# Moving loop, softmax and output operands to other offsets modulo 256 bytes, and one rotation from GpSimd to VectorE, in a hybrid attention block

## The chip, the cores and the metric

The kernel runs on one core of a Trainium2 chip. The metric is the device time of one execution in microseconds. Three timed executions of the kernel before took 802.62, 804.39 and 804.96 us, a median of 804.39 us. One more execution was recorded by the hardware profiler; it took 802.8 us, of which 801.0 us lie between the first and the last instruction (the span).

## The reference, cut to what matters

The block normalises x (512 tokens, 2048 columns), projects it with one matrix `w_in`, runs two groups of attention heads on the result, gates the heads' outputs with a SiLU, multiplies by `w_out`, adds x and normalises once more.

```python
h = _rmsnorm(x, norm_g[l])
proj = h @ w_in[l]
...
qa = _rope(_heads(qa, N_HEADS_A, HEAD_DIM_A))
kc = _compress(_rope(kca), cmp_k_pos, cmp_k_w1, cmp_k_w2)
vc = _compress(vca, cmp_v_pos, cmp_v_w1, cmp_v_w2)
o_a = gates[0] * o_cmp + gates[1] * o_sel + gates[2] * o_win
y_a = o_a * silu(za)
...
o_b = _banded_attention(qb, _rope(kb), vb, WIN_B, sink)
y_b = o_b * silu(zb)
x = x + concatenate([y_a, y_b]) @ w_out
return _rmsnorm(x, final_g)
```

Group A has 8 heads of 128 columns (compressed, selected and window attention), group B 16 heads of 64 columns with a window of 128 tokens and a sink. All products are float32.

## The kernel before

**How a product is made.** A float32 operand is kept as two words, a high one (`h`, rounded) and the remainder (`l`). `mm3` (L118 to L121) makes one product out of three matmuls: high by high, then high by low, then low by high; the scheduler may change their order. A matmul streams its second operand (the moving one, 256 or 512 columns here) past its first operand (the stationary one, 128 columns), which a weight load has put into the array before. A `pe.transpose` is a matmul too: it streams the identity `ident` (128 columns) past the tile that is transposed.

**The stages, in order of time.** Projection of group B and its attention (to 291 us): matmuls of 512 columns that stream `xh`/`xl` past weight words, and between them the scores (L349, L350), transposes (L384) and outputs (L389, L390) of `softmax_b` and `attn_b`. The value loops: for u in 0 to 3, `tok_chunk` (256 columns, weights moving, x stationary) makes the values of `wv1`, and after each chunk come two `compress_unit` calls of 8 matmuls each (L708, L709; weights moving, `F` stationary); then for u in 0 to 7 the same with 280 columns of `wv0` and one `compress_unit`. Then `seven` (L570 on) makes each head's query and gate from seven half-size products of 256 columns (`prod`, L551): the x words `pu`, `qw`, `xh`, `xl` move, the weight words stand still. Eight heads follow each other; `attn_a` of head h (scores L932, transposes L969, L981, L983, outputs L975 to L977, L990, L992) is interleaved by the scheduler with the products of `pair(h + 1)`. Last, from about 620 us, the product with `w_out`: the words of y stand still and the weight words move (L1153 on and `product`, L1254).

**Where the words lie.** `words(place)` gives a pair of weight words out of tiles of 1088 columns; `place` shifts the use inside the tile, so that the 1024 columns used begin at another offset. `MOVING, EVEN, STILL, BELOW = 0, 16, 32, 48` columns are 0, 64, 128 and 192 bytes. Adding up the tiles in the order of their pools gives each operand's address; the table has it modulo 256 bytes.

| operand | before | after |
|---|---|---|
| weight words at MOVING / EVEN / STILL / BELOW | 128 / 192 / 0 / 64 | the same, BELOW no longer used |
| `xh`, `xl`, `pu`, `qw` | 192 | 192 |
| `KH`, `KL` (from their first column) | 192 | 192 |
| `qh`, `ql`, `qs` | 0 | 0 |
| `ident` | 128 | 192 |
| `F`, `ph`, `pl`, `pcr`, `pd` | 128 | 192 |
| `VH`, `VL`, `VC`, `VF`, `VB`, `tt0`, `tt1`, `pc`, `ttb` | 192 | 0 |
| words of y (`yh`, `yl`, and `p`, `q`, `u` of `combos`) | 192 | 0 |

In what follows **the step** from one matmul to the next is the address of the next stationary operand minus the address of the current moving operand, modulo 256 bytes. Inside each loop of the kernel before the step is 64: the value loops have 192 - 128, `compress_unit` 128 - 64, the heads' products 0 - 192, an attention output 192 - 128, the output stage 192 - 128.

**The single steps.** `step` (L125 to L127) issues one matmul of 256 columns at the end of a stage whose result is overwritten; its operands are chosen by address alone. There are three: before the value loops (L828), through `seven` in `keys(0)` (L635) and before the last part of the output stage (L1168).

**Head 0's rotation.** `pair(h)` (L671) takes the query half of `seven`, rotates it in `turn` (L658 to L666: two half products and a product on VectorE, then an addition) and splits it in `q_split` (L257: high word on ScalarE, low word a subtraction). For h below 6 the addition (L664) and the subtraction (L261) run on GpSimd. The query tile `t1` has one buffer, so the next head's first write into it, the ScalarE copy at L608, follows the subtraction.

Of the kernel before, what the change touches and what calls it, by code (L numbers as in the profile page):

```python
# [27 lines left out]
CMP = 32  # L28
MOVING, EVEN, STILL, BELOW = 0, 16, 32, 48
WARM = 40  # L30
# [5 lines left out]
def hybrid_block(ctx, tc, xT, xtm, w0, wv0, wv1, wz, wq, wo0, wos, cw1, cw2, cpos, e2, rope, tabs, sinks, gT, fg, out):  # L36
# [5 lines left out]

    const = ctx.enter_context(sb("const"))
    wp = ctx.enter_context(sb("wp", bufs=3))
    ident = const.tile([P, P], F32, name="ident")
# [4 lines left out]
    bmask = tab[:, 512 + NQ * CMP:768 + NQ * CMP]  # L50
    small = const.tile([P, 8], F32, name="small")
    rstd, eps = small[:, 0:NQ], small[:, NQ:NQ + 1]
    rstdb = const.tile([P, S], F32, name="rstdb")
    gates = const.tile([P, NQ, 24], F32, name="gates")
    gt = const.tile([P, KT + 1], F32, name="gt")
    rowvalid = gt[:, KT:KT + 1]

# [49 lines left out]
    xpool = ctx.enter_context(sb("xpool", side="right"))  # L107
    xh = xpool.tile([P, KT, S], F32R, name="xh")
    xl = xpool.tile([P, KT, S], F32R, name="xl")
    angles = xstack.enter_context(sb("angles", side="right"))  # L110
# [11 lines left out]

    flat = xh.rearrange("p k s -> p (k s)")

# [19 lines left out]
    def load_x(k):  # L144
        xr = tmp("xr")
        if k == 0:
            nc.sync.dma_start(gt, gT)
        nc.sync.dma_start(xr, xT[:, k, :])
        last["xh"] = act.activation(xh[:, k, :], xr, AF.Copy, scale=gt[:, k:k + 1]).ins
        return xr  # L150
# [48 lines left out]
    with tc.issue_after(last["dma"]):  # L199
        nc.sync.dma_start(cosB, rope[:, 2, :])  # L200
        nc.sync.dma_start(sinB, rope[:, 3, :])
        nc.sync.dma_start(tab, tabs)
    dve.tensor_tensor(out=cosB, in0=cosB, in1=rstdb, op=ALU.mult)
    dve.tensor_tensor(out=sinB, in0=sinB, in1=rstdb, op=ALU.mult)
# [86 lines left out]

    vbf = wb.tile([P, NQ, P], F32, name="vbf")
    sk = wb.tile([P, 5, 16], F32, name="sk")
    nc.sync.dma_start(sk[:, 0, :], sinks)
    act.activation(sk[:, 1, :], sk[:, 0, :], AF.Copy, scale=-1.0)
    KBH = wb.tile([P, 2, S], F32R, name="KBH")
    KBL = wb.tile([P, 2, S], F32R, name="KBL")
    VB = wb.tile([P, NQ, 2, P], F32R, name="VB")
# [34 lines left out]
    def softmax_b(i, q2):  # L333
        g = i // 4
        tts = []
        skb = sk[:, 0, 2 * i:2 * i + 2].unsqueeze(1).to_broadcast([P, 2, 2])
        nskb = sk[:, 1, 2 * i:2 * i + 2].unsqueeze(1).to_broadcast([P, 2, 2])
        for part in range(2):
            sums = wk.tile([P, 3, 2, 2], F32, name="sums", tag="sums")
            mn, dn, ex = sums[:, 0], sums[:, 1], sums[:, 2]  # L340
            for e in range(2):
                qt = 2 * part + e
                tt = wb.tile([P, 2, 256], F32, name="ttb", tag="ttb", bufs=6)
                tts.append(tt)
                ko = max(qt - 1, 0) * P
                qs = slice(qt * P, (qt + 1) * P)
                sp = pssb.tile([P, 2, 256], F32, name="spb", tag="spb")
                for v in range(2):
                    pe.matmul(sp[:, v, :], q2[v][:, qs], KBH[:, g, ko:ko + 256], start=v == 0, stop=False)  # L349
                    pe.matmul(sp[:, v, :], q2[v][:, qs], KBL[:, g, ko:ko + 256], start=False, stop=v == 1)  # L350
                n = 256 if qt else 128
                for v in range(2):
                    dve.tensor_tensor_reduce(out=tt[:, v, 0:n], in0=sp[:, v, 0:n], in1=bmask[:, 256 - n:256],
                                             scale=-SCALE_B, scalar=1e38, op0=ALU.add, op1=ALU.min,
                                             accum_out=mn[:, e, v:v + 1])
            dve.tensor_tensor(out=mn, in0=mn, in1=nskb, op=ALU.min)  # L356
            dve.tensor_tensor(out=ex, in0=mn, in1=skb, op=ALU.add)
            act.activation(ex, ex, AF.Exp)
            for e in range(2):
                n = 256 if part or e else 128  # L360
                for v in range(2):
                    tv = tts[2 * part + e][:, v, 0:n]
                    act.activation(tv, tv, AF.Exp, bias=mn[:, e, v:v + 1], scale=-1.0, accum_out=dn[:, e, v:v + 1])  # L363
            dve.tensor_tensor(out=dn, in0=dn, in1=ex, op=ALU.add)
            dve.reciprocal(dn, dn)
            for e in range(2):
                n = 256 if part or e else 128
                for v in range(2):
                    tv = tts[2 * part + e][:, v, 0:n]
                    dve.tensor_scalar(tv, tv, dn[:, e, v:v + 1], None, op0=ALU.mult)  # L370
        return tts
# [124 lines left out]
    VF = kv.tile([P, 2, 2, 256], F32, name="VF")  # L496
    VC = [kv.tile([P, P], F32R, name=f"VC{g}") for g in range(2)]
    ahead = ExitStack()
    quarters = [ahead.enter_context(sb(f"ahead{e}", side="right")).tile([P, 1024], F32, name=f"ahead{e}") for e in range(2)]
# [171 lines left out]
    def pair(h, hooks=None, extra=None):  # L671
        def q_done(qv):
            turn(qv, engine=pool if h < 6 else dve)
            return q_split(qv, pool if h < 6 else dve)

# [142 lines left out]
    early, ready = quarters[:1], quarters[1:]  # L818
    places = [words(MOVING), words(BELOW), words(BELOW)]

# [24 lines left out]
    for u in range(8):  # L845
# [5 lines left out]
        if u == 0:  # L851
# [3 lines left out]
            cacc[1] = bank(4)  # L855
        compress_unit(1, u, cacc[1], words(BELOW))
        if 1 <= u <= 3:
# [28 lines left out]
    kv = kvstack.enter_context(sb("kvK", side="right"))  # L886
    KH, KL = [kv.tile([P, CMP + 1056], F32R, name=f"K{e}")[:, 0:CMP + 1024] for e in "HL"]
    for e, k in enumerate((KH, KL)):
        act.activation(k[:, 0:CMP], k0w[:, e].bitcast(F32), AF.Copy)
# [19 lines left out]
    def attn_a(h, qh, ql, st):  # L909
# [4 lines left out]
        for pair in range(2):  # L914
            tt = wa.tile([P, 1792 if pair else 768], F32, name=f"tt{pair}", tag=f"tt{pair}")
            sums = wk.tile([P, 2, 2, 3], F32, name="sums", tag="sums")
            mn, dn = sums[:, 0], sums[:, 1]
# [82 lines left out]

    yh, yl = [[w[:, (2 * f + 1) % 17, :] for f in range(16)] for w in (xh, xl)]

# [148 lines left out]
    for c, u, ms in ((0, 0, ()), (0, 1, ()), (0, 2, ()), (1, 0, (0, 1, 2)), (1, 1, (3, 4)), (1, 2, (5, 6)), (0, 3, ()),  # L1151
                     (1, 3, (7,))):
        hi, lo = load_unit(wo0[:, c, u], 1024, place=MOVING, loaded=first_units.pop(0) if first_units else None, after=last["qh"],  # L1153
                           after_lo=low_y[11] if (c, u) == (0, 2) else last["turn"])
# [9 lines left out]
        with tc.issue_after(words_of), tc.issue_after(last["gate", 1]):  # L1164
            for m in ms:
                combos(m)
    banks1 = banks(1)
    step(banks1[3], flat[:, 3 * S - 16:3 * S + 112], flat[:, 2 * S + 32:2 * S + 288])  # L1168
    for T in range(2):
# [30 lines left out]
    def halves(raw, to=None):  # L1200
        hi, lo = to or words(MOVING)
        split_to(hi, lo, raw)
# [6 lines left out]
    for n in range(1, 4):  # L1209
# [117 lines left out]
        else:  # L1327
# [8 lines left out]
            def pair():  # L1336
                return words(MOVING)

# [181 lines left out]
```

## Time and profile before

| what | us |
|---|---|
| timed executions, median (lowest to highest) | 804.39 (802.62 to 804.96) |
| the profiled execution / its span | 802.8 / 801.0 |
| TensorE busy in matmuls | 789.6 (99%), 5693 matmuls |
| weight loads | 739.1 (92%) |
| VectorE / ScalarE / GpSimd | 686.3 / 504.7 / 108.3 |
| DMA | 131.05 MB, mean 164 GB/s |

A profile page has one line for each engine's busy time, 40 slices of the span, the chain of work that ended last, and groups of instructions with the mean duration of one. Further views are used below: windows (busy time and number of instructions between two times), timelines (start, duration, engine, line, operation, written tile <- read tiles, shape), and waits. Matmuls are pipelined: one of 256 columns is shown with a duration of about 0.28 us, and the next one starts 0.11 to 0.12 us after it. So a window counts about two matmuls more than start in it, and the distance between starts, not the duration, is what a matmul costs.

### The profile page before, as it was taken

What the parts mean: (1) busy time and instruction counts of PE and PEld (TensorE: products, weight loads), DVE (VectorE), ACT (ScalarE), POOL (GpSimd) and SP (SyncE); (2) the same over time, 40 slices, a digit from 0 to 9 for tenths busy, and PEclk for the clock granted to TensorE, in tenths of its full rate; (3) what the DMA queues carried; (4) which work ended last, traced back from release to release, by engine and by line L of the source; (5) the groups of instructions that cost most, each with busy time, mean ns of one, the idle gap of its engine ahead of it and who ended that gap; (6) DMA issues with size and microseconds to landing.
All of it is one profiled execution on the core that took longest, in us unless ns stands there. A gap on an engine that the chain in (4) does not pass through costs nothing.

```text
span 801.0 us, 15316 instructions
## 1 busy us (share of the span) xinstructions
PE 789.6 (99%) x5693; PEld 739.1 (92%) x5693; DVE 686.3 (86%) x1407; ACT 504.7 (63%) x1103; POOL 108.3 (14%) x111
## 2 busy tenths in 40 slices
PE   9999999999999999999999999999999999999996
PEld 8788888888888899999999999999999999999996
DVE  7668988889989597759999999998999798978895
ACT  6646657655666356664447778777777867553545
POOL 3615002110121000323210110110100000000000
PEclk9999999999999999999999999999999999999998
DMA  7572243564373469887723213225216836797845
GB/s 239 172 242 81 79 144 106 171 171 150 101 210 106 158 200 281 257 269 194 207 82 106 68 53 119 82 92 159 71 50 216 296 120 219 257 266 193 258 86 211
DMA packets 49563, 131.05 MB, mean 164 GB/s; under 512 B 6000, under 2 KB 8848, under 8 KB 49488
## 3 DMA queue, kind: packets, MB, share of 16 engines
q1 hardware_dynamic: 43376, 110.89, 42.3%
q0 software_dynamic: 5824, 18.65, 10.5%
q8 instruction: 45, 0.74, 0.4%
q10 hardware_dynamic: 288, 0.52, 0.2%
q14 instruction: 30, 0.25, 0.1%
HBM read 113.23 MB, written 16.81 MB: 162 GB/s over the span
## 4 chain that ended last, share of the span: by engine, by line
PE 86%; DVE 6%; DMA 3%; ACT 2%; issue 2%; POOL 0%; SPq 0%; DVEq 0%; ACTq 0%
PE pj L119 16%; PE pj L121 15%; PE pj L120 15%; PE oa L120 5%; PE oa L119 5%; PE oa L121 5%; PE sp L932 4%; PE bank L121 2%; PE bank L120 2%; PE bank L119 2%; DMA xr<-xT 2%; DVE wlo L543 2%; PE tp L969 2%; PE tp L384 2%; DMA raw<-wq 1%
## 5 line engine op out<-in xcount | busy, mean ns | idle before, releaser
L119 PE MATMUL pj<-xh,whi 128*128 128x256 f32 (+1 forms) x592 | 196.9, 333 | 0.6 <-ACT t L608 0.5
L121 PE MATMUL pj<-xh,wlo 128*128 128x256 f32 (+1 forms) x592 | 196.2, 331 | 0.0
L120 PE MATMUL pj<-xl,whi 128*128 128x256 f32 (+1 forms) x592 | 196.1, 331 | 0.0
L119 PEld LDWEIGHTS pj<-xh,whi 128*128 128x128 f32 x592 | 111.4, 188 | 11.0 <-ACT t L608 0.9
L121 PEld LDWEIGHTS pj<-xh,wlo 128*128 128x128 f32 x592 | 111.4, 188 | 10.1
L120 PEld LDWEIGHTS pj<-xl,whi 128*128 128x128 f32 x592 | 111.4, 188 | 9.7
L543 DVE TENSOR_TENSOR wlo<-raw,whi 128x1024 fp32r<-128x1024 f32 (+2 forms) x80 | 92.9, 1172 | 7.8 <-ACT whi L542 7.2
L542 ACT ACTIVATE whi<-raw 128x1024 fp32r<-128x1024 f32 (+2 forms) x80 | 77.6, 985 | 30.7 <-DVE raw L581 11.5
L99 DVE TENSOR_TENSOR wlo<-raw,whi 128x1024 fp32r<-128x1024 f32 (+1 forms) x61 | 72.1, 1184 | 22.8 <-ACT whi L97 22.3
L97 ACT ACTIVATE whi<-raw 128x1024 fp32r<-128x1024 f32 (+1 forms) x60 | 56.6, 945 | 28.8 <-PE pj L120 14.8
L120 PE MATMUL oa<-wlo,xh 128*128 128x256 f32 x200 | 55.5, 278 | 0.0
L119 PE MATMUL oa<-whi,xh 128*128 128x256 f32 x200 | 55.4, 278 | 0.0
L121 PE MATMUL oa<-whi,xl 128*128 128x256 f32 x200 | 55.2, 276 | 0.0
L121 PE MATMUL pj<-pu,wlo 128*128 128x256 f32 x160 | 45.0, 281 | 0.5 <-DVE wlo L543 0.5
L119 PE MATMUL pj<-pu,whi 128*128 128x256 f32 x160 | 45.1, 282 | 0.4 <-DVE zr L581 0.4
L120 PE MATMUL pj<-pu,whi 128*128 128x256 f32 x160 | 44.7, 279 | 0.0
L289 DVE TENSOR_TENSOR pl<-tp,ph 128x512 fp32r<-128x512 f32 (+1 forms) x64 | 40.7, 651 | 3.1 <-ACT ph L288 2.9
L288 ACT ACTIVATE ph<-tp 128x512 fp32r<-128x512 f32 (+1 forms) x64 | 34.1, 560 | 9.6 <-PE tp L969 4.4
L363 ACT ACTIVATE ttb<-ttb,sums 128x256 f32<-128x256 f32 (+1 forms) x64 | 30.0, 471 | 14.4 <-DVE sums L356 14.4
L121 PEld LDWEIGHTS oa<-whi,xl 128*128 128x128 f32 x200 | 37.6, 188 | 0.0
L120 PEld LDWEIGHTS oa<-wlo,xh 128*128 128x128 f32 x200 | 37.6, 188 | 0.0
L119 PEld LDWEIGHTS oa<-whi,xh 128*128 128x128 f32 x200 | 37.5, 188 | 0.0
(401 smaller groups left out, 2369.8 us busy)
## 6 DMA issues: line engine op xcount, KB each, us to landing
raw<-wq SPq DMA_DIRECT2D x41, 512.0 KB, 4.4
raw<-wz SPq DMA_DIRECT2D x36, 512.0 KB, 4.0
cw<-cw SPq DMA_DIRECT2D x32, 256.0 KB, 4.0
raw<-wos SPq DMA_DIRECT2D x14, 512.0 KB, 5.9
rw<-wos SPq DMA_DIRECT2D x10, 512.0 KB, 4.8
xr<-xT SPq DMA_DIRECT2D x16, 256.0 KB, 3.4
rows<-xT SPq DMA_DIRECT2D x8, 512.0 KB, 4.7
raw<-wo SPq DMA_DIRECT2D x8, 512.0 KB, 6.0
```

The source lines that it names most:

```text
L97: last["hi"] = act.activation(hi[:, :width], rw[:, :width], AF.Copy).ins
L99: last["lo"] = dve.tensor_tensor(out=lo[:, :width], in0=rw[:, :width], in1=hi[:, :width].bitcast(F32), op=ALU.subtract).ins
L119: pe.matmul(ps, ah, bh, start=first, stop=False, skip_group_check=go_on)
L120: pe.matmul(ps, ah, bl, start=False, stop=False, skip_group_check=go_on)
L121: recent["mm"] = pe.matmul(ps, al, bh, start=False, stop=last, skip_group_check=go_on).ins
L288: act.activation(ph, tp, AF.Copy)
L289: dve.tensor_tensor(out=pl, in0=tp, in1=ph.bitcast(F32), op=ALU.subtract)
L363: act.activation(tv, tv, AF.Exp, bias=mn[:, e, v:v + 1], scale=-1.0, accum_out=dn[:, e, v:v + 1])
L384: pe.transpose(tp[:, o:o + P], tts[kt + s][:, v, c0:c0 + P], ident)
L542: split_hi = act.activation(hi, src, AF.Copy).ins
L543: last["lo"] = dve.tensor_tensor(out=lo, in0=src, in1=hi.bitcast(F32), op=ALU.subtract).ins
L932: pe.matmul(sp[:, a:b], qq[:, qs], kk[:, ko:ko + b - a], start=pi == 0, stop=pi == 2)
```

## The change

It has three parts.

1. Tiles get another size, another order or padding, so that the addresses in the table above go from the left column to the right one. `compress_unit` gets its words at MOVING rather than BELOW, and the output stage at EVEN rather than MOVING. The third `step` gets other operands. `vbf` shares a buffer with `ob`. With that the steps between a loop and the work that interrupts it become 64 as well: products and attention outputs, products and transposes, value chunks and compress units.
2. `rowvalid` moves from the tile `gt` to `small` and gets a DMA of its own (128 rows of 4 bytes on SyncE's queue, after the one of `tabs`).
3. In `pair`, head 0's addition (L664) and subtraction (L261) go from GpSimd to VectorE.

```diff
-MOVING, EVEN, STILL, BELOW = 0, 16, 32, 48
+MOVING, EVEN, STILL = 0, 16, 32
...
+    gt = const.tile([P, KT], F32, name="gt")
...
-    small = const.tile([P, 8], F32, name="small")
+    small = const.tile([P, 16], F32, name="small")
...
-    gt = const.tile([P, KT + 1], F32, name="gt")
-    rowvalid = gt[:, KT:KT + 1]
+    rowvalid = small[:, 8:9]
...
-    xh = xpool.tile([P, KT, S], F32R, name="xh")
-    xl = xpool.tile([P, KT, S], F32R, name="xl")
+    slabs = xpool.tile([P, 2 * KT * S + 64], F32R, name="x")
+    xh, xl = [slabs[:, e * KT * S:(e + 1) * KT * S].rearrange("p (k s) -> p k s", s=S) for e in range(2)]
...
+        nc.sync.dma_start(rowvalid, gT[:, KT:KT + 1])
...
-    vbf = wb.tile([P, NQ, P], F32, name="vbf")
+    vbf = wb.tile([P, NQ, P], F32, name="vbf", tag="ob")
+    KBH = wb.tile([P, 2, S], F32R, name="KBH")
+    KBL = wb.tile([P, 2, S], F32R, name="KBL")
     sk = wb.tile([P, 5, 16], F32, name="sk")
...
-            sums = wk.tile([P, 3, 2, 2], F32, name="sums", tag="sums")
+            sums = wk.tile([P, 6, 2, 2], F32, name="sums", tag="sums")
...
     VC = [kv.tile([P, P], F32R, name=f"VC{g}") for g in range(2)]
+    kv.tile([P, 48], F32, name="space")
...
-            turn(qv, engine=pool if h < 6 else dve)
-            return q_split(qv, pool if h < 6 else dve)
+            turn(qv, engine=pool if 0 < h < 6 else dve)
+            return q_split(qv, pool if 0 < h < 6 else dve)
...
-    places = [words(MOVING), words(BELOW), words(BELOW)]
+    places = [words(MOVING) for n in range(3)]
...
-        compress_unit(1, u, cacc[1], words(BELOW))
+        compress_unit(1, u, cacc[1], words(MOVING))
...
     KH, KL = [kv.tile([P, CMP + 1056], F32R, name=f"K{e}")[:, 0:CMP + 1024] for e in "HL"]
+    kv.tile([P, 16], F32, name="space")
...
-    yh, yl = [[w[:, (2 * f + 1) % 17, :] for f in range(16)] for w in (xh, xl)]
+    yh, yl = [[slabs[:, (e * KT + (2 * f + 1) % 17) * S + 16:][:, 0:S] for f in range(16)] for e in range(2)]
...
-        hi, lo = load_unit(wo0[:, c, u], 1024, place=MOVING, loaded=first_units.pop(0) if first_units else None, after=last["qh"],
+        hi, lo = load_unit(wo0[:, c, u], 1024, place=EVEN, loaded=first_units.pop(0) if first_units else None, after=last["qh"],
...
+    cmb.tile([P, 48], F32, name="space3")
     banks1 = banks(1)
-    step(banks1[3], flat[:, 3 * S - 16:3 * S + 112], flat[:, 2 * S + 32:2 * S + 288])
+    step(banks1[3], flat[:, 2 * S:2 * S + P], flat[:, 3 * S - 16:3 * S + 240])
...
-        hi, lo = to or words(MOVING)
+        hi, lo = to or words(EVEN)
...
             def pair():
-                return words(MOVING)
+                return words(EVEN)
```

More of the change, by code (lines that the diff above doesn't have):

```diff
@@ L121, in mm3 @@
         recent["mm"] = pe.matmul(ps, al, bh, start=False, stop=last, skip_group_check=go_on).ins
-    flat = xh.rearrange("p k s -> p (k s)")
+    flat = slabs[:, 0:KT * S]
     def step(bank, still, moving):
@@ L146, in load_x @@
         if k == 0:
-            nc.sync.dma_start(gt, gT)
+            nc.sync.dma_start(gt, gT[:, 0:KT])
         nc.sync.dma_start(xr, xT[:, k, :])
@@ L295, in hybrid_block @@
     act.activation(sk[:, 1, :], sk[:, 0, :], AF.Copy, scale=-1.0)
-    KBH = wb.tile([P, 2, S], F32R, name="KBH")
-    KBL = wb.tile([P, 2, S], F32R, name="KBL")
     VB = wb.tile([P, NQ, 2, P], F32R, name="VB")
@@ L915, in attn_a @@
             tt = wa.tile([P, 1792 if pair else 768], F32, name=f"tt{pair}", tag=f"tt{pair}")
-            sums = wk.tile([P, 2, 2, 3], F32, name="sums", tag="sums")
+            sums = wk.tile([P, 4, 2, 3], F32, name="sums", tag="sums")
             mn, dn = sums[:, 0], sums[:, 1]
```

## The prediction

> **What bounds the kernel now.** The page first, then the stages as windows.
>
> ```profile
> span 801.0 us, 15316 instructions
> PE 789.6 (99%) x5693; PEld 739.1 (92%) x5693; DVE 686.3 (86%) x1407; ACT 504.7 (63%) x1103; POOL 108.3 (14%) x111
> ...
> 291.10:320.40 29.30, 29.30 (x252) 29.29 (x251) 24.16 (x68) 18.89 (x45) 0.87 (x1) 1.00 0.87 260
> 390.40:429.00 38.60, 38.08 (x329) 37.68 (x328) 38.08 (x58) 19.11 (x31) 4.43 (x4) 1.00 0.39 112
> 429.00:620.00 191.00, 190.79 (x1602) 188.66 (x1601) 180.41 (x389) 148.31 (x371) 16.30 (x10) 1.00 0.32 104
> 620.00:678.70 58.70, 58.70 (x510) 58.43 (x509) 49.52 (x127) 43.78 (x105) 0.00 (x0) 1.00 0.60 215
> ```
>
> The columns of a window are its length, then busy time and instructions of TensorE, its weight loads, VectorE, ScalarE and GpSimd, then granted clock, DMA share and GB/s. TensorE is busy 99% of the span and at clock 1.00 in these stages. So time is won only where matmuls follow each other faster, or where one of its few waits goes (the one that the change touches stands below, under head 0). How fast they follow is not the same everywhere:
>
> ```profile
> 298.30:303.50 5.20, 5.20 (x46) 1.00 0.96 316
> 678.80:786.00 107.20, 107.20 (x948) 1.00 0.74 209
> ```
>
> Both hold matmuls of 256 columns alone, at the same clock. A window counts about two more than start in it. The second gives 107.20 / 946 = 113.3 ns a matmul, the first 5.20 / 44 = 118 ns. I call these the **fast** and the **slow spacing**; they differ by 4.5 ns (4%). Both stretches have steps of 64 throughout, so the step alone does not choose between them. The timeline shows what switches:
>
> ```profile
> 303.48 0.28 PE L121 MATMUL bank<-whi,xl 128*128 128x256 f32 x1
> 303.60 0.29 PE L708 MATMUL pj<-whi,F 128*128 128x256 f32 x1
> ...
> 304.07 0.28 PE L708 MATMUL pj<-whi,F 128*128 128x256 f32 x1
> ...
> 305.32 0.28 PE L709 MATMUL pj<-wlo,F 128*128 128x256 f32 x1
> 305.43 0.28 PE L119 MATMUL bank<-whi,xh 128*128 128x256 f32 x1
> ```
>
> From 304.07 to 305.32 eleven matmuls take 1.25 us: 114 ns, fast. Before 303.48 the value chunk was slow, and after 305.43 the next one is slow again. At 303.48 the step is 0 (from `whi` at 128 to `F` at 128), at 305.32 it is 128 (from BELOW at 64 to `xh` at 192). Reading all such places with settled neighbours from the timeline (the first at 295.88, the last at 572.38): a step other than 64 changes the spacing in 12 cases of 13, while steps of 64 kept a fast stretch fast 1914 times of 1914. So **the spacing is something that steps of 64 keep and other steps flip**, and the three `step` matmuls (own steps 0 and 128, and at 291.11 entered from 512 columns) each set it to fast. Mean durations per group carry the same mark:
>
> ```profile
> L120 PE MATMUL bank<-wlo,xh 128*128 128x256 f32 x62 | 17.4, 281 | 0.0
> L121 PE MATMUL oa<-whi,xl 128*128 128x256 f32 x137 | 37.8, 276 | 0.0
> L121 PE MATMUL pj<-xh,wlo 128*128 128x256 f32 x200 | 56.1, 281 | 0.0
> L975 PE MATMUL op<-ph,VH 128*128 128x256 f32 x50 | 14.1, 282 | 0.0
> ```
>
> 276 ns is the fast spacing (row two, window 678.8 to 786), 281 the slow one: row one is the value chunks (291.1 to 320.4), rows three and four are products and outputs in the heads' stage (429 to 620).
>
> **The change part by part**, against the profiled execution's 802.8 us.
>
> *Value loops (291 to 320).* 250 matmuls start there: at 113.3 ns they would need 28.4 us of the 29.3; 0.8 us is lost to the slow spacing. After the change chunk and `compress_unit` have steps of 64 on both sides, so the fast spacing set at 291.11 should last. One matmul in this stage waited:
>
> ```profile
> 298.12 0.34 PE L120 MATMUL bank<-wlo,xh 128*128 128x256 f32 x1
> 298.30 0.28 PE L121 MATMUL bank<-whi,xl 128*128 128x256 f32 x1
> ```
>
> It takes 180 ns to the next start, 60 too many; if that drops the spacing to slow, the remaining 190 stay slow with nothing to flip them back. Ends: 0.8 gained; 250 x 4.5 = 1.1 spent where 0.8 was, 0.3 lost. I take **-0.5**, nearer to the gain, because the next chunks' spacing decides most.
>
> *The 280-column loop (320 to 353).* A matmul of 280 columns ends 96 bytes further modulo 256, so its spacing drifts by itself. Only the 64 compress matmuls can gain: 0.2 us at most, or lose as much. **-0.1**.
>
> *Heads' stage (429 to 620).* Products are interrupted by outputs (steps 0 in, 128 out), transposes (0 in, 128 out) and scores. 1282 matmuls of 256 columns start there; those that do not follow a wait or a transpose lose 3.2 us to the slow spacing and to settling. The change makes the visits to outputs and transposes 64 both ways. Outputs then no longer flip anything. Transposes are different:
>
> ```profile
> 429.30:434.40 5.10, 5.10 (x47) 1.00 0.60 182
> 487.95:493.10 5.15, 5.15 (x45) 1.00 0.61 206
> ...
> 648.66 0.38 PE L969 MATMUL tp<-ident,tt 128*128 128x128 f32 x2
> 648.80 0.36 PE L120 MATMUL oa<-wlo,xh 128*128 128x256 f32 x1
> 649.00 0.28 PE L121 MATMUL oa<-whi,xl 128*128 128x256 f32 x1
> ```
>
> The first two are long stretches that begin after scores: about 45 and 43 matmuls, at 113 and 119 ns, so one fast and one slow. The matmul behind transposes starts the next one 200 ns later, and the spacing it lands in looks like a coin: of 57 stretches whose entry can be read in this stage (the first at 429.30, the last at 615.25), 25 begin fast, 32 slow. Eight visits in the output stage, between 620.68 and 663.59, already had steps of 64 on both sides of the transposes: 3 landed fast, 4 slow, 1 unreadable. So I keep the coin, let each stretch hold the spacing with which it began, and get 445 slow matmuls x 4.5, 39 in stretches too short to read x 4 and 25 settlings x 8 ns: 2.4 us where 3.05 (scores left out) were. **-0.65**. Ends: all fast, -3.2; all slow, 1200 x 4.5 = 5.4 where 3.2 were, +2.2. Scores into the second column group of `KH` keep their step of 192; that is not changed.
>
> *First output units (620 to 678).* Here the step from scores to products goes from 128 to 192. With 128, five landings of six were fast; with 192, in the heads' stage, 9 of 17. Three stretches of about 45 lose half their chance: **+0.25** (ends -0.45, all of what is lost there now, and +1.5).
>
> *Rest of the output stage.* Fast now; the new third `step` has the same steps around it (0 in, 128 out) and the form of the one at 390.43, which entered from a slow stretch and left fast. **0**; if it failed, 946 x 4.5 = +4.2.
>
> *Group B (74 to 291).* The 182 matmuls of 256 columns lose 0.7 us now. Scores L349 keep their entry step of 64 and are mostly slow with it (118 ns); outputs L389 get the same entry. **0**, ends -0.7 and +0.3.
>
> *`rowvalid`'s DMA, `vbf` in `ob`'s buffer, the padding.* One more issue on SyncE's queue at 50 us, behind which weight loads run a unit ahead; `rowvalid` is read after 350 us, and `ob` is first written a head later than `vbf` is read. **0**; at worst one issue late, under 0.1.
>
> *Head 0 on VectorE.*
>
> ```profile
> 416.61 1.28 POOL L664 TENSOR_TENSOR t<-t,t 128x512 f32<-128x512 f32 x1 [21.54 <-DVE t L662]
> 418.64 1.49 POOL L261 TENSOR_TENSOR ql<-t,qh 128x512 fp32r<-128x512 f32 x1 [0.75 <-ACT qh L260]
> ...
> 414.63 1.23 DVE L543 TENSOR_TENSOR wlo<-raw,whi 128x1024 fp32r<-128x1024 f32 x1
> 415.77 0.69 DVE L662 TENSOR_TENSOR t<-t,cosA 128x512 f32<-128x512 f32 x1
> 416.70 2.27 DVE L543 TENSOR_TENSOR wlo<-raw,whi 128x1024 fp32r<-128x1024 f32 x1
> 418.90 1.78 DVE L677 TENSOR_TENSOR zr<-zr,rstdb 128x512 f32<-128x512 f32 x1
> ...
> 421.25 0.36 ACT L608 ACTIVATE t<-pj 128x256 f32<-128x256 f32 x1
> ...
> 420.85 0.29 PE L932 MATMUL sp<-KH,ql 128*128 128x288 f32 x1
> 421.66 0.39 PE L119 MATMUL pj<-xh,whi 128*128 128x256 f32 x1 [0.52 <-ACT t L608]
> ```
>
> TensorE starts nothing between 420.85 and 421.66: 0.81 instead of 0.13 us, 0.68 lost, until L608 has copied. L608 stands on ScalarE behind the SiLU that waits for L677. While GpSimd works, VectorE's subtraction takes 2.27 instead of 1.23 us and L677 1.78 instead of 0.69: 2.1 us of stretching. The change gives VectorE two instructions of 128x512 at 0.69 us, 1.4 us. The subtraction there waits for ScalarE's high word (0.64 us after the addition); L543 fits between them, and L677 and the sums of the next head stand behind. L677 then ends at about 420.68 - 2.1 + 1.4 = 420.0, L608 at about 420.95, when TensorE is just done. The stall goes: **-0.6**. The other end: the stretching has another cause and stays. Then L677 and all behind it are 1.4 us late in a stage in which VectorE is busy 38.08 of 38.60 us, and the stall grows by as much, +1.4.
>
> Sum: -0.5 - 0.1 - 0.65 + 0.25 - 0.6 = **-1.6 us**. The four executions shown lie at 802.62, 802.8, 804.39 and 804.96; the profiled one is a low one, and the middle of the four is 803.6. I put the new time at 803.6 - 1.6 = **802.0 us**, 0.3% under the median given; the gain itself is 0.2%.
>
> **The rivals.**
> 1. *Transposes keep the spacing too*, once all steps around them are 64. Then the heads' stage stays fast from the `step` at 390.43 except behind scores: -2.6 there, -0.8 and -0.2 in the loops, -0.2 in the first output units, -0.6 for head 0: -4.4, **799.2**. For it: steps of 64 kept the spacing in every settled case. Against it: the eight visits above.
> 2. *Addresses have no effect*, and the two spacings have another cause (what is written, or the queue). Then only head 0 counts: **803.0**. For it: the stretches at 429.30 and 487.95 have the same steps and are fast and slow, so something beside the step takes part. The Trainium skill speaks for this: SBUF — State Buffer, section "A bandwidth-pool intuition that's wrong (but worth ruling out)", gives TensorE a second, independent read port for weight loads, so where the two operands lie should not matter; and TensorE: Matmul & The Clock Gate, section "Back-to-back issue gap", has one isolated spacing for 256 columns, 256 / 2.4 + 2.5 = 109 ns as an estimate. The trace does not agree with one spacing: it has 113.3 and 118 at clock 1.00, and the flips stand where the addresses jump.
> 3. *The last `step` lands slow.* Slower than before: nothing flips the spacing back before 786 us, so +4.2 - 1.6 = +2.6, **806.2**. It decides from the first dozen matmuls after it. For it: these operands have not run in this place. Against it: three of three steps with 128 out led to fast.
>
> **How the numbers follow.** Forecast 0.50, rival 1 0.25, rival 2 0.15, rival 3 0.10. A measurement tells 0.3%, 2.4 us, from no change. The coin of some 57 stretches, each 20 matmuls x 4.5 ns, spreads by 0.7 us, with the long ones and a reordered schedule by about 1.2; so a quarter of the forecast's cases gain over 2.4 us (0.12), with nearly all of rival 1 (0.24): faster 0.36. Slower: most of rival 3 and a little of the rest, 0.09. Same 0.55. The range leaves out rival 3 and the deepest cases of rival 1: **798.8 to 805.0**.
>
> **What would show it.** Windows of the value loops: 250 matmuls in 28.4 us and group means of 276 ns; no flip at the borders of L708. Outputs L975 with the same mean as the products around them. Stretches after transposes still half slow (else rival 1). No wait for L608 at about 421 us, no GpSimd rows there, L543 at 1.2 us. The window after the third `step` at 113.3 ns. The forecast is wrong if the value loops keep 281 ns, or if the heads' stage moves by more than 2 us either way.

## The result and the profile after

The changed kernel took 813.49 us (median of four executions, 812.11 to 817.96), the kernel before 804.38 beside it. The ratio is 1.0127, with a 95% interval of 1.0084 to 1.0169. The prediction said 802.0 us and a range of 798.8 to 805.0: it is wrong by 11.5 us and in sign. Six more executions (run `e11_change_again` below) had a median of 811.75 us, ratio 1.0097 [1.0076, 1.0118].

The profile page of the changed kernel, its first lines and the shares of the chain that ended last:

```profile
span 816.2 us, 15335 instructions
...
PE 799.2 (98%) x5693; PEld 744.1 (91%) x5693; DVE 681.9 (84%) x1409; ACT 504.3 (62%) x1103; POOL 105.0 (13%) x109
...
PE 59%; DVE 22%; DMA 7%; ACT 6%; issue 5%; SPq 0%; POOL 0%; ACTq 0%; POOLq 0%; DVEq 0%
```

The profiled execution is the slowest of the four (817.96). VectorE has less busy time than before (681.9 for 686.3), yet its share of the chain rose from 6% to 22%: TensorE now waits for it. The same line of the kernel before:

```profile
PE 86%; DVE 6%; DMA 3%; ACT 2%; issue 2%; POOL 0%; SPq 0%; DVEq 0%; ACTq 0%
```

The windows say where TensorE waits (columns as in the prediction):

```profile
429.00:620.00 191.00, 187.35 (x1556) 183.22 (x1555) 173.52 (x376) 142.57 (x355) 15.95 (x10) 1.00 0.30 95
620.00:678.70 58.70, 58.46 (x497) 57.87 (x497) 46.54 (x117) 41.70 (x102) 0.00 (x0) 1.00 0.56 196
696.00:786.00 90.00, 90.00 (x766) 90.00 (x765) 75.13 (x89) 44.31 (x61) 8.55 (x10) 1.00 0.75 205
```

Row one, the heads' stage: TensorE stands idle for 3.65 us where it was 0.21, and 46 fewer of its matmuls fit (1556 for 1602). VectorE is busy for 173.52 instead of 180.41 us in the same length, so it stands idle for longer as well (17.5 us for 10.6). Row three is the output stage: 90.00 us for 764 starts are **117.8 ns** a matmul, the slow spacing, where before had the fast one throughout. The waits view of TensorE (waited for, us in total, times, longest) names the rest:

```profile
PE pj L121 <- DVE wlo L545: 2.0, 4, 0.8
PE pj L119 <- ACT whi L544: 1.2, 2, 0.8
...
PE pj L119 <- ACT x L1050: 1.1, 1, 1.1
...
PE oa L120 <- DVE wlo L1055: 0.7, 1, 0.7
```

(L544 and L545 are the weight words' split, L542 and L543 before; L1050 and L1055 make y words, L1047 and L1052 before.)

**How I count.** Two sums are used below, both from the starts of all matmuls in a trace. *Waits*: where the next start comes more than 45 ns later than the length of the matmul asks for (229 ns for 512 columns, 130 for 288, 129 for 280, 115.5 for 256, 109 for 128, and 87 more for the first one behind matmuls of 128 columns), that excess, from 60 us on. *Slow spacing*: what each unbroken stretch of 256-column matmuls takes over 113.3 ns a matmul. For before they are 5.6 and 5.2 us, for the changed kernel 15.5 and 10.3. So 9.9 of the 15.2 us of longer span are waits and 5.1 are slow spacing, 4.3 of these in one stretch. Not all of the waits come with the change. Up to the scores of head 0 (420.2 us in before) TensorE's row is the same in all traces of this document, and the waits there vary from about 3 to 6 us (before 3.7, the change 5.5). From there on before has 1.8 us and the change 9.7.

**Where the waits come from.** The scheduler, which lays out every engine's instructions from its own estimate of their times, gave the changed program another order from head 0 on (424 us). TensorE's row is that of before for the first 2543 matmuls. Of the whole rows, the longest part that stands in the same order in both is 90% on TensorE, 87% on VectorE and 88% on ScalarE. The timeline shows what that means. Head 1's scores before the change:

```profile
445.40 0.38 PE L932 MATMUL sp<-KH,qh 128*128 128x288 f32 x1
445.62 0.29 PE L932 MATMUL sp<-KL,qh 128*128 128x288 f32 x1
445.75 0.28 PE L121 MATMUL pj<-pu,wlo 128*128 128x256 f32 x1
...
446.77 0.28 PE L121 MATMUL pj<-pu,wlo 128*128 128x256 f32 x1
446.89 0.29 PE L932 MATMUL sp<-KH,ql 128*128 128x288 f32 x1
```

and after it, with GpSimd's two rows for the same head:

```profile
443.19 2.13 POOL L666 TENSOR_TENSOR t<-t,t 128x512 f32<-128x512 f32 x1 [45.90 <-DVE t L664]
446.06 2.08 POOL L262 TENSOR_TENSOR ql<-t,qh 128x512 fp32r<-128x512 f32 x1 [0.74 <-ACT qh L261]
...
447.66 0.29 PE L935 MATMUL sp<-KL,qh 128*128 128x288 f32 x1
448.20 0.40 PE L935 MATMUL sp<-KH,ql 128*128 128x288 f32 x1 [0.25 <-POOL ql L262]
448.82 0.39 PE L979 MATMUL op<-pl,VH 128*128 128x256 f32 x1 [0.22 <-DVE pl L290]
```

In the old order ten products stood between the second score and the third, which needs the low word `ql` that GpSimd makes last. In the new one the third score follows at once and waits for `ql`, then the output waits for `pl`, while products that need neither stand behind them. TensorE takes its matmuls in the order given. The Trainium skill states that too (TensorE: Matmul & The Clock Gate, section "The mechanism": matmuls start and end strictly in order), and the rows agree: 0.54 and 0.62 us from start to start instead of 0.13.

The longest wait is at the end of the heads:

```profile
675.85 2.26 ACT L1054 ACTIVATE ph<-yp 128x256 fp32r<-128x256 f32 x7 [2.74 <-PE op L995]
678.01 1.05 ACT L1054 ACTIVATE whi<-raw 128x1024 fp32r<-128x1024 f32 x1
678.96 1.94 ACT L1054 ACTIVATE uh<-yp 128x256 fp32r<-128x256 f32 x6
...
680.12 0.28 PE L121 MATMUL pj<-whi,x 128*128 128x256 f32 x1
...
680.80 0.61 ACT L1050 ACTIVATE x<-yp 128x512 fp32r<-128x512 f32 x1
...
681.47 0.39 PE L119 MATMUL pj<-whi,x 128*128 128x256 f32 x1 [1.06 <-ACT x L1050]
```

Head 7's outputs end at 675.8 us, and ScalarE then has 14 copies ahead of the y word that TensorE wants at 680.2. Before, ScalarE had as many ahead of that word:

```profile
664.23 2.26 ACT L1051 ACTIVATE ph<-yp 128x256 fp32r<-128x256 f32 x7 [1.67 <-PE op L992]
666.40 2.25 ACT L1051 ACTIVATE uh<-yp 128x256 fp32r<-128x256 f32 x7
668.55 0.62 ACT L1047 ACTIVATE xh<-yp 128x512 fp32r<-128x512 f32 x1
```

But 33 matmuls of the output units stood between the last outputs and the product with that word (664.0 to 667.8 us), and TensorE never waited for it. Now there are 3.

**Where the 4.3 us come from:**

```profile
694.49 0.28 PE L121 MATMUL oa<-whi,pl 128*128 128x256 f32 x1
695.46 0.39 PE L120 MATMUL oa<-wlo,x 128*128 128x256 f32 x1 [0.69 <-DVE wlo L1055]
695.68 0.28 PE L121 MATMUL oa<-whi,x 128*128 128x256 f32 x1
```

The third `step`, 49 matmuls earlier, had set the fast spacing (5.59 us for these 49, 114 ns). The stretch behind this wait is slow, and with steps of 64 and no wait behind it all its 957 matmuls stay so: 957 x 4.5 ns = 4.3 us.

### The profile page after: what moved, and what is told of

The parts are those of the page before. It is cut to its first block, busy times and chain, and to the rows that moved or that the text cites. A ratio compares the mean times of both kernels' runs of the same rounds, so it can differ in the third digit from the quotient of the medians.

```text
span 816.2 us, 15335 instructions
## 1 busy us (share of the span) xinstructions
PE 799.2 (98%) x5693; PEld 744.1 (91%) x5693; DVE 681.9 (84%) x1409; ACT 504.3 (62%) x1103; POOL 105.0 (13%) x109
## 3 DMA queue, kind: packets, MB, share of 16 engines
q0 software_dynamic: 5824, 18.65, 10.4%
## 4 chain that ended last, share of the span: by engine, by line
PE 59%; DVE 22%; DMA 7%; ACT 6%; issue 5%; SPq 0%; POOL 0%; ACTq 0%; POOLq 0%; DVEq 0%
PE pj L121 9%; PE pj L119 9%; PE pj L120 9%; PE oa L120 4%; PE oa L121 4%; PE oa L119 4%; DVE wlo L545 3%; PE bank L120 3%; PE bank L121 3%; PE bank L119 2%; PE sp L935 2%; DMA yw<-st 2%; DVE wlo L99 2%; DMA raw<-wq 2%; DVE qs L330 2%
## 5 line engine op out<-in xcount | busy, mean ns | idle before, releaser
L119 PE MATMUL pj<-x,whi 128*128 128x256 f32 (+1 forms) x592 | 197.1, 333 | 0.5 <-ACT whi L544 0.4
L121 PE MATMUL pj<-x,wlo 128*128 128x256 f32 (+1 forms) x592 | 196.4, 332 | 0.8 <-DVE wlo L545 0.8
L120 PE MATMUL pj<-x,whi 128*128 128x256 f32 (+1 forms) x592 | 196.4, 332 | 0.0
L121 PEld LDWEIGHTS pj<-x,wlo 128*128 128x128 f32 x592 | 111.5, 188 | 11.0 <-DVE wlo L545 1.0
L119 PEld LDWEIGHTS pj<-x,whi 128*128 128x128 f32 x592 | 111.4, 188 | 10.8 <-ACT whi L544 0.6
L120 PEld LDWEIGHTS pj<-x,whi 128*128 128x128 f32 x592 | 111.6, 188 | 9.8
L545 DVE TENSOR_TENSOR wlo<-raw,whi 128x1024 fp32r<-128x1024 f32 (+2 forms) x80 | 90.9, 1149 | 9.3 <-ACT whi L544 8.8
L544 ACT ACTIVATE whi<-raw 128x1024 fp32r<-128x1024 f32 (+2 forms) x80 | 77.3, 983 | 21.8 <-DVE raw L583 8.6
L99 DVE TENSOR_TENSOR wlo<-raw,whi 128x1024 fp32r<-128x1024 f32 (+1 forms) x61 | 72.2, 1185 | 17.5 <-ACT whi L97 17.2
L120 PE MATMUL oa<-wlo,x 128*128 128x256 f32 x200 | 56.3, 282 | 0.7 <-DVE wlo L1055 0.7
L121 PE MATMUL oa<-whi,x 128*128 128x256 f32 x200 | 56.1, 281 | 0.0
L119 PE MATMUL oa<-whi,x 128*128 128x256 f32 x200 | 56.0, 281 | 0.0
L120 PEld LDWEIGHTS oa<-wlo,x 128*128 128x128 f32 x200 | 37.6, 188 | 0.9 <-DVE wlo L1055 0.9
L119 PEld LDWEIGHTS oa<-whi,x 128*128 128x128 f32 x200 | 38.1, 191 | 0.0
L121 PEld LDWEIGHTS oa<-whi,x 128*128 128x128 f32 x200 | 37.6, 188 | 0.0
```

The lines of the kernel that those rows point to most:

```text
L99: last["lo"] = dve.tensor_tensor(out=lo[:, :width], in0=rw[:, :width], in1=hi[:, :width].bitcast(F32), op=ALU.subtract).ins
L119: pe.matmul(ps, ah, bh, start=first, stop=False, skip_group_check=go_on)
L120: pe.matmul(ps, ah, bl, start=False, stop=False, skip_group_check=go_on)
L121: recent["mm"] = pe.matmul(ps, al, bh, start=False, stop=last, skip_group_check=go_on).ins
L544: split_hi = act.activation(hi, src, AF.Copy).ins
L545: last["lo"] = dve.tensor_tensor(out=lo, in0=src, in1=hi.bitcast(F32), op=ALU.subtract).ins
```

## The experiments

Theories: **order** (the scheduler's new order makes the waits), **load** (VectorE, full in the heads' stage, can't take two instructions more) and **placement** (the new places, or the one tile for all x words, make the waits or the slow spacing). All times are medians with their range, the kernel before measured beside each group.

| run | what it is | us (range, executions) | before | ratio, 95% | span of the profile | waits | slow spacing |
|---|---|---|---|---|---|---|---|
| before | | | 804.38 | | 801.0 | 5.6 | 5.2 |
| after | the change | 813.49 (812.11-817.96, 4) | 804.38 | 1.0127 [1.0084, 1.0169] | 816.2 | 15.5 | 10.3 |
| e1 | placement alone, old order | 803.97 (802.79-806.20, 12) | 803.71 | 1.0008 [0.9997, 1.0019] | 801.0 | 5.2 | 6.0 |
| e2 | head 0 alone, new order | 812.43 (810.67-817.70, 6) | 803.71 | 1.0129 [1.0100, 1.0158] | 810.1 | 13.4 | 6.3 |
| e3 | the change, old order | 803.20 (801.98-805.05, 12) | 803.71 | 0.9999 [0.9987, 1.0010] | 803.3 | 7.8 | 5.5 |
| e4 | before, new order | 821.09 (819.55-824.26, 5) | 803.71 | 1.0229 [1.0204, 1.0254] | 819.0 | 18.5 | 10.4 |
| e5 | the change and a late step | 812.30 (811.22-814.69, 6) | 803.18 | 1.0113 [1.0093, 1.0132] | 812.9 | 15.3 | 7.5 |
| e6 | only TensorE in the old order | 807.58 (806.33-813.65, 7) | 803.18 | 1.0063 [1.0038, 1.0087] | 805.8 | 9.5 | 6.2 |
| e7 | only VectorE and ScalarE in it | 807.22 (806.37-809.52, 6) | 803.18 | 1.0050 [1.0030, 1.0070] | 805.0 | 8.8 | 5.8 |
| e8 | only the addition on VectorE | 808.23 (806.34-809.45, 6) | 803.18 | 1.0055 [1.0036, 1.0074] | 806.4 | 9.8 | 6.2 |
| e9 | head 0 alone, old order | 803.32 (801.99-807.80, 12) | 803.42 | 1.0001 [0.9985, 1.0017] | 800.4 | 5.2 | 4.7 |
| e10 | e9 and the value loops' places | 802.91 (801.03-805.11, 12) | 803.42 | 0.9986 [0.9970, 1.0002] | 799.7 | 4.7 | 4.6 |
| e11 | the change again | 811.75 (810.32-814.63, 6) | 804.07 | 1.0097 [1.0076, 1.0118] | 810.6 | 14.8 | 6.0 |
| e12 | e5 again | 812.01 (811.01-813.59, 6) | 804.07 | 1.0102 [1.0083, 1.0122] | 809.6 | 13.9 | 5.8 |

The last three columns close: span less waits less slow spacing is 789.8 to 790.5 us in all fourteen traces, so whatever these kernels differ by is one of the two.

**Placement alone, and head 0 alone (e1, e2).** The first puts head 0 back on GpSimd in the changed kernel, and the scheduler then gives exactly the order of before. The second changes two lines of the kernel before and gets exactly the changed kernel's order.

```diff
e1, in the changed kernel:
-            turn(qv, engine=pool if 0 < h < 6 else dve)
-            return q_split(qv, pool if 0 < h < 6 else dve)
+            turn(qv, engine=pool if h < 6 else dve)
+            return q_split(qv, pool if h < 6 else dve)
e2, in the kernel before: the reverse
```

> Parts 1 and 2 of the change alone; head 0's addition and subtraction stay on GpSimd, and every engine keeps the order of the kernel before. Order theory (the time was lost because the program's scheduler put the work of all engines into another order once head 0 moved): 802 to 804 us, about 1 us under before, TensorE's waits after 60 us near the 5.6 us of before. Placement theory (the new places and the shared tile for the x words make waits, or upset the spacing): 810 to 814 us. Load theory (two more instructions on a VectorE that is already full in the heads' stage): 802 to 804 us.

> Part 3 alone: head 0's addition and subtraction on VectorE in the kernel before, with its own places; the scheduler then gives TensorE, VectorE and ScalarE the order that the changed kernel has. Order theory: 808 to 814 us, with some 10 us more of TensorE's waits than before, most of them from 440 to 700 us; the output stage is at 118 ns a matmul only if a wait there drops it. Load theory: the same 808 to 814. Placement theory: 803 to 804.5 us.

Placement alone costs nothing that can be measured (804.0, no gain either), head 0 alone costs all of it (812.4). Placement as the cause of the loss is out.

**Order or load (e3, e4).** Order and engine are parted by holding every engine to a stated order. A list of instruction numbers, taken from another kernel, becomes a chain on each engine:

```python
def in_stated_order(tc):
    ...
    for n in names:
        i = traced[f"I-{n}"]
        if i.engine in before:
            tc.add_manual_dep(i, before[i.engine], mybir.DependencyInfo(
                mybir.DependencyClass.NoSync, mybir.DependencyReason.DATA), reason="stated order")
        before[i.engine] = i.name
```

In e3 it is the order of before for the changed kernel, with head 0's addition behind `v * cosA` and its subtraction behind the next L543. In e4 it is the new order for the kernel before, with the two instructions put back into GpSimd's row. Not quite everything is held: the 160 VectorE instructions that add the masks to the scores and take their minima (`tensor_tensor_reduce`, CUSTOM in the timelines) are not in the list. In the traces of e3, e4, e9 and e10 some of these stand elsewhere than in the kernel whose order is stated; all other VectorE and ScalarE instructions and all matmuls stand as stated.

> The whole change, but every engine is held to the order of the kernel before; only the two instructions of head 0 are put into VectorE's row, where the prediction had them. Order theory: the prediction's own case, 801 to 803 us, no wait over 0.4 us in the heads' stage, 113.3 ns in the output stage, and no stall at about 421 us. Load theory: 806 us or more, with waits for VectorE from 420 us on. Placement theory: 810 to 814 us.

> The kernel before with its own places and head 0's rotation on GpSimd, but every engine is held to the order that the scheduler gave after the change; the two instructions are put back into GpSimd's row. Order theory: 808 to 814 us, as slow as part 3 alone. Load theory: 803 to 805 us, since VectorE has the load of before. Placement theory: 803 to 805 us.

This decides it. The whole change, in the order of before, takes 803.2 us; the kernel before, in the new order, takes 821.1. The load theory wanted 806 or more and 803 to 805. Windows of the heads' stage, e3 and then e4:

```profile
429.00:620.00 191.00, 190.79 (x1600) 188.28 (x1599) 180.48 (x389) 148.47 (x369) 16.16 (x10) 1.00 0.33 103
```

```profile
429.00:620.00 191.00, 184.80 (x1529) 180.78 (x1528) 171.99 (x369) 139.96 (x346) 14.77 (x10) 1.00 0.29 92
```

With the old order TensorE idles for 0.21 us, exactly as before; with the new one and less work for VectorE it idles for 6.2. The order theory's ranges were missed all the same: e3 lies 0.2 us over its range (its 2.2 us of waits more than before all stand ahead of the scores of head 0), and e4 far over it.

Counted from the scores of head 0 on, the waits are 1.5 to 1.8 us in the five traces of the old order (before, e1, e3, e9, e10) and 9.5 to 10.2 us in the five of the new one with head 0 on VectorE (the change, e2, e5, e11, e12). So the new order costs about 8 us, whatever the places, and holding an order costs nothing that shows, since e3, e9 and e10 are held.

That e4 is worse than e2 by 8.7 us I had not expected. The profiles differ by 8.9 us, 4.1 of slow spacing and 5.1 of waits:

```profile
607.62 2.36 DVE L611 TENSOR_TENSOR wlo<-raw,whi 128x1024 fp32r<-128x1024 f32 x2 [2.22 <-ACT whi L610]
609.89 0.18 DVE L1002 CUSTOM_DVE_ANT_0 tc__7150<-sp,tab 128x32 f32<-128x32 f32 x1
...
610.92 0.61 PE L1000 MATMUL sp<-KH,qh 128*128 128x288 f32 x2 [2.46 <-DVE sums L1006]
...
699.00:786.00 87.00, 87.00 (x741) 87.00 (x741) 72.13 (x86) 42.98 (x60) 7.69 (x9) 1.00 0.74 206
```

The first three rows show one wait of 2.6 us that e2 doesn't have: L1002 and L1006, which follows it at once, are free VectorE instructions and stand behind two weight splits here, in e2 ahead of them. Another 0.7 is head 0's old stall behind its third score, and 1.7 stand ahead of head 0. The last row is the output stage behind the wait that the change has at 694.49 us (697.24 here). It is slow, 739 starts in 87.00 us or 117.7 ns, with the places of before, so the slow stretch isn't tied to the new ones.

**Whose order (e6, e7).** The same chain on TensorE alone, or on VectorE and ScalarE alone; the scheduler fits the rest around it.

> The whole change; only TensorE is held to the order of the kernel before, the other engines are ordered by the scheduler (their rows then nearly agree with those of before). If TensorE's own order makes the waits: 802 to 804.5 us. If the rows of VectorE and ScalarE make them, and these rows' small remaining differences count: 806 us or more.

> The whole change; VectorE and ScalarE are held to the order of the kernel before, TensorE is ordered by the scheduler. If TensorE's own order makes the waits: 806 to 814 us, with TensorE waiting for VectorE or ScalarE in the heads' stage. If the rows of VectorE and ScalarE make them: 802 to 804.5 us.

Both come out between the two orders, at +4.4 and +4.0 us, and each in its upper range: by e6 the small differences left in the rows of VectorE and ScalarE count, by e7 TensorE's own order does. In e6 the free rows of VectorE and ScalarE agree with those of e3 by 99%, and still TensorE waits for 3.4 us between 449 and 458 us (for `tt`, `ph` and `pl`). In e7 it is one score that waits 1.1 us for `ql` at 479, and smaller ones. So no single engine's row is the cause: the rows of the engines belong together.

**Half the work (e8).** Only the addition goes to VectorE, in a free order, which is a third one.

> The changed kernel with head 0's subtraction back on GpSimd, the addition still on VectorE, ordered freely by the scheduler, which gives a third order (TensorE's agrees with neither kernel's from head 0 on). If any reordering costs waits (the order of before is an unusually good one): 807 us or more, though half the work was moved. If what counts is the load moved: about half of the loss, 804 to 809, and less than with both.

808.2 us, +5.0: somewhat over half the loss for half the work, but by the order theory's number too. It doesn't tell order and load apart; e3 and e4 do. Every order tried that isn't that of before (the new one in the change, e2 and e4, and those of e6, e7 and e8) is slower, by 4 to 17 us.

**The late step (e5, e11, e12).** One more single matmul behind the first product behind the wait, and the change itself again for its spread:

```diff
             product(bb, [halves(r) for r in r22], "22", True)
         if n == 1:
+            step(banks1[3], flat[:, 2 * S:2 * S + P], flat[:, 3 * S - 16:3 * S + 240])
             first_rows()
```

> The changed kernel with one more single matmul of the kind of the third `step`, 48 matmuls behind the place where the profiled execution waited at 694.49 us; every engine keeps the changed kernel's order. Locked-spacing theory (the 4.3 us that the profiled execution lost from 695.68 us on are one unlucky landing after a wait, which some executions have and others not): from the new matmul on 113.3 ns in the profile whatever the stretch before it shows, all executions between 810 and 814.5 us, none at 816 to 818. If the 4.3 us have another cause: the stretch stays at 117.8 ns in the profile, or some executions still take 816 to 818 us.

> The changed kernel itself, for the spread of its executions. Locked-spacing theory: most executions from 811 to 814.5 us, about one in four 3 to 5 us higher, because the wait at about 694.5 us lands it at 118 ns for the 957 matmuls behind it; the profile shows which of the two it was. If the spread has another cause: no gap between two groups, or a high execution with 113.3 ns there.

> The changed kernel with the late step, on the same chip. Locked-spacing theory: the lower group alone, 811 to 814.7 us, and 113.3 ns behind the late step whatever stands before it. If the spread has another cause: the same spread as without the step.

The window 696 to 786 us of e11, to be held against the one of the change above:

```profile
696.00:786.00 90.00, 90.00 (x797) 90.00 (x796) 77.47 (x91) 45.38 (x62) 8.55 (x10) 1.00 0.76 205
```

The same program, the same wait at the same place (0.88 us here, 0.85 there), and this time it lands fast: 795 starts in 90.00 us, 113.2 ns. So one program can have either spacing behind this wait, and 4.3 of the 5.6 us between the two spans are that. How often it is slow isn't shown. One of the change's ten executions and two of e2's six stood some 5 us above their medians, and with the late step none of twelve did (one, 814.69, is 0.2 us over its range); but the kernel before, which doesn't have this wait, also has executions 3 to 4 us above its median (807.15, 807.41), so a time alone doesn't tell the cause. In both profiles with the late step the stretch before it was already fast, so that this step would have turned a slow one round was not seen. For the third `step` it was: in the change, e5 and e8 it follows a stretch at 117.8 ns and leaves 113.3, once settled.

**What is left of the gains (e9, e10).** e9 is head 0 alone in the old order. e10 adds, of all placements, only the value loops':

```diff
-        F = wk.tile([P, 4, P], F32R, name="F", tag=("ph", "pl")[u % 2])
+        F = wk.tile([P, 576], F32R, name="F", tag=("ph", "pl")[u % 2])[:, 16:528].rearrange("p (j q) -> p j q", q=P)
...
-    places = [words(MOVING), words(BELOW), words(BELOW)]
+    places = [words(MOVING) for n in range(3)]
...
-        compress_unit(1, u, cacc[1], words(BELOW))
+        compress_unit(1, u, cacc[1], words(MOVING))
```

> The kernel before with its own places; head 0's addition and subtraction on VectorE, every engine held to the order of before. Order theory, with the prediction's own term for head 0: 0.6 to 0.7 us under before, 802.8 to 803.4 us, no wait of TensorE at 421 us, L543 there at 1.2 us. Load theory: 804 us or more, since VectorE is late by 1.4 us from 421 us on.

> As the last one, and of the placements only the value loops': `compress_unit` with its words at MOVING and `F` 64 bytes further on (its buffers 256 bytes wider, `vbf` in `ob`'s buffer for the room). Only the 128 matmuls of the compress units get other addresses, those from 620 us on keep theirs. If the placements gain 0.7 us in the value loops and lose 0.8 in the first output units: 1.3 to 1.4 us under before, 802.0 to 802.6 us, ratio 0.998, and faster than any other kernel here. If the value loops' gain is paid back elsewhere in any case: as the last one.

The profiled spans fall as expected, 800.4 and 799.7 us after 801.0, but each is one execution among the faster of its kernel. The timed ratios don't resolve it: 1.0001, and 0.9986 with 1 just inside its interval; e10's median of 802.91 misses its range by 0.3 us. The load theory's 804 or more for e9 didn't come either. e10 has the lowest median of all these kernels, and it is over 1% under the changed one; that it beats the kernel before is likely, not shown.

## Why the prediction was wrong, step by step

**The step that failed** is the one that let every other term be read from the trace of before: that head 0's move leaves the order of the work around it as it is. The text has "a reordered schedule" once, inside a spread of about 1.2 us. It cost about 8 us of waits: from the scores of head 0 on 9.7 us in the change and 10.0 in e2, where before has 1.8 and the change in the old order (e3) 1.5. The rest of the loss in the profiled execution is mainly the slow stretch of 4.3 us. Nothing in the profile of before shows how a scheduler will lay out the next version, but it shows what a bad layout can lose: 0.2 us of idle time in 191 us of the heads' stage, at 94% for VectorE, is a fit with no slack. With the order held, the prediction's own case is e3, and that came out at 803.2 us for 802.0, level with the kernel before beside it (0.9999 [0.9987, 1.0010]). So the forecast gain of 1.6 us isn't there either, mainly because the placements gained nothing in sum (below).

**Rival 3** had the right price (+4.2 forecast, 4.3 measured) and the right place, with the wrong trigger: the `step` itself landed fast in every trace, and a wait 49 matmuls later, which the old order doesn't have, did the damage in the profiled execution.

The other terms, by slow spacing in the stage (us), before, then the two runs with all new places in the old order:

| term | forecast | before | e1 | e3 | measured |
|---|---|---|---|---|---|
| value loops | -0.5 (-0.8 to +0.3) | 0.76 | 0.04 | 0.04 | -0.7 |
| 280-column loop | -0.1 | 0.14 | 0.18 | 0.17 | 0.0 |
| heads' stage, 429 to 620 | -0.65 (-3.2 to +2.2) | 2.61 | 2.62 | 2.61 | 0.0 |
| first output units | +0.25 (-0.45 to +1.5) | 0.43 | 1.31 | 1.27 | +0.9 |
| rest of the output stage | 0 | 0.02 | 0.01 | 0.06 | 0.0 |
| group B | 0 | 0.45 | 0.43 | 0.42 | 0.0 |

*Value loops*: right, and toward the good end. The windows 299 to 319 us of before and of e1 (TensorE alone):

```profile
299.00:319.00 20.00, 20.00 (x173) 1.00 0.95 282
```

```profile
299.00:319.00 20.00, 20.00 (x179) 1.00 0.94 279
```

171 starts in 20.00 us (117 ns) became 177 (113), and no compress unit flips the spacing any more. The loss of before varies too: e2 and e9, with the old places there, have 0.65 and 0.51 us. And the bad end occurs: in e5 and e8 a wait in the stage dropped the spacing and nothing brought it back (0.86 us), as the prediction feared.

*First output units* ate it: five stretches of 23 to 66 matmuls there, 219 in all, are slow in e1 and in e3, and the same five were fast before. The forecast had the direction, not the size. From 353 to 429 us, for which it had no term, before has 0.8 us, e1 1.5 and e3 0.9, the difference being one landing behind a wait. So all placements together, forecast at -1.0, came out at +0.3 to +0.8.

*Heads' stage*: visits to outputs no longer flip, but the landings behind transposes and scores came out no better. That refutes rival 1, and the sum was right to keep the coin, but it isn't one (see the last section).

*Rival 2* (addresses have no effect): refuted. Before and e1 differ in addresses (and `rowvalid`'s DMA) alone, order and engines being the same, and the value loops change their spacing, as do 23 of 59 stretches behind transposes and scores (last section; with the same places it is 1 of 58). The Trainium skill (SBUF — State Buffer, "A bandwidth-pool intuition that's wrong (but worth ruling out)") gives weight loads a read port of their own. That where the operands lie should not matter was the prediction's inference from it, not the page's statement, and these two traces refute the inference.

*Head 0*: the mechanism was right to a tenth of a microsecond, in e3 (its lines stand 68 further down: L613 is L545, L734 and L330 head 0's addition and subtraction, L747 and L678 what the prediction calls L677 and L608):

```profile
418.65 0.69 DVE L734 TENSOR_TENSOR t<-t,t 128x512 f32<-128x512 f32 x1
...
419.59 1.22 DVE L613 TENSOR_TENSOR wlo<-raw,whi 128x1024 fp32r<-128x1024 f32 x1
420.73 0.68 DVE L330 TENSOR_TENSOR ql<-t,qh 128x512 fp32r<-128x512 f32 x1
421.33 0.68 DVE L747 TENSOR_TENSOR zr<-zr,rstdb 128x512 f32<-128x512 f32 x1
...
422.58 0.37 ACT L678 ACTIVATE t<-pj 128x256 f32<-128x256 f32 x1
...
423.00 0.29 PE L1003 MATMUL sp<-KH,ql 128*128 128x288 f32 x1
423.13 0.28 PE L187 MATMUL pj<-x,whi 128*128 128x256 f32 x1
```

The stretching is gone (1.22 and 0.68 us for 2.27 and 1.78), the multiply with `rstdb` ends 1.0 us ahead of the third score (0.85 forecast) and the stall is 0.13 instead of 0.81 us. On the clock it is worth less: the stall with GpSimd was only 0.37 in e1's trace, so 0.2 to 0.7 us, under what these runs resolve. In the scheduler's own order the subtraction stands behind two instructions more; e5, e11 and e12 keep 0.47 us there, the change's own trace 0.13.

The rows of the prediction also fit one cause of the stretching. L543 started at 416.70, GpSimd's addition ended at 417.89, and 1.22 us behind that is 419.1; L543 ended at 418.97. For L677 the same sum gives 420.13 + 0.69 = 420.8, and it ended at 420.68. The Trainium skill's rule (SBUF — State Buffer, section "Who interferes with whom": VectorE and GpSimd share one port pair as a lock, and the loser waits for the whole instruction) fits both rows within 0.15 us.

**Open:** why the scheduler prefers an order that is 1% slower isn't in any trace; that its estimate of some instruction is off is only a guess.

## What to carry to other kernels

In a kernel whose order is laid out by a scheduler, moving one small instruction to another engine is a change of the whole order behind it: compare the engines' rows of the two programs before pricing the instruction, and if they differ, treat a tightly packed stage as at risk by several times the edit's own worth. A good order is worth holding: chaining each engine to the known row kept 803 us under an edit that otherwise cost 9. Where a speed is set once and kept by what follows, look for the last wait behind the place that sets it, since one wait can undo it for the whole stretch.

## What the runs showed of the hardware

- **The landings are no coin.** I had read the spacing behind transposes and scores as chance (25 fast, 32 slow). Between 425 and 680 us e1 and e3 have TensorE's row and the places in common, and all 58 stretches of five matmuls or more that follow a transpose or a score have the same spacing in both traces. Before and e9, also alike there, agree in 57 of 58, and the one that differs follows a wait. Before and e1, with the same order and other places, agree in 36 of 59. So without waits the spacing follows from addresses and sequence, by a rule that steps of 64 alone don't give. In the new order, with its waits, two executions of one program (the change and e11) agree in 39 of 46.
- **Behind a wait it can come out either way.** The same program had 117.8 ns in one execution (the change) and 113.2 in another (e11) behind the wait at 694.5 us, over 90 us each time. Behind the wait at 518.4 us, 0.94 us long in both, it had 117.8 and 113.4 over 58 matmuls. The record doesn't say whether the two executions ran on the same chip.
- A wait costs more than the engine's idle time: behind 181 of the 198 waits of over 0.15 us in the fourteen traces the next start comes late too, mostly by 0.08 or 0.11 us (695.46 to 695.68 is 0.22 us).
